# Cross-attention in a two-block network: the queries of heads 2 and 3 as one unit of seven block products, with the sums of token blocks made beside the first four query tiles

## The chip, the cores and the metric

The kernel runs on one core of a Trainium2 chip as one program. The metric is the device time of an execution in microseconds (us); lower is better. The engines that matter are PE (TensorE, the matrix engine), DVE (VectorE), ACT (ScalarE), POOL (GpSimd, used here to issue DMAs that add to what lies in SBUF) and SP (SyncE, which issues the plain loads). Each engine takes its instructions strictly in the order in which the program has them; an instruction that waits for a semaphore holds up all that stand behind it on the same engine.

## The reference, cut to what matters

The network is two blocks in a row on 512 tokens of width 1024. The change touches the cross-attention of the second block, which reads a memory of 256 rows:

```python
def cross_attention(xn, memn, w_q, w_kv, w_o):
    q = (xn @ w_q).reshape(b, s, XATTN_HEADS, XATTN_HEAD_DIM)      # 512 tokens, 4 heads of 256
    k, v = jnp.split(memn @ w_kv, 2, axis=-1)
    ...
    scores = jnp.einsum('bqhd,bkhd->bhqk', q, k).astype(jnp.float32) * (XATTN_HEAD_DIM ** -0.5)
    p = jax.nn.softmax(scores, axis=-1).astype(v.dtype)
    o = jnp.einsum('bhqk,bkhd->bqhd', p, v).reshape(b, s, D_MODEL)
    return o @ w_o
```

The order of the whole is: feed-forward 1, mixer 1, feed-forward 2, mixer 2, cross-attention, squared-ReLU MLP, last norm.

## The kernel before

Activations lie with their features on the 128 partitions and the 512 tokens in the free direction, so the residual is eight tiles `x[0]` to `x[7]` of 128x512, and a linear layer gives its output in tiles of 128 features. Every operand of a matmul is split into a high part and a low part: ACT casts (`L322` for activations, `L269` or `L162` for a weight tile of 128x1024) and DVE subtracts (`L323`, `L270`, `L163`). A product of two split operands takes three matmuls, high by high, high by low and low by high (`mm3`, L278).

A query tile is `q_lin(i)`: `linear` loads one weight tile (SP, 512 KB), splits it, runs 24 matmuls with 512 columns (8 blocks of the depth by 3), and `split_x` splits the result. Tiles 0 and 1 (head 0) have their matmuls in two halves of 256 columns. Two tiles make a head of width 256.

`head(hd)` is a generator. Its first two steps each put the scores of two token blocks into a PSUM tile (`x`, 12 matmuls of 256 columns), take the maximum on DVE (L1377, L1378), the exponential on ACT (L1381), and the reciprocal and the scaling on DVE (L1384, L1387). The third step transposes the probabilities on PE (L1395), splits them, and, for head 0, splits four tiles of V (`L322` and `L323` with 128x512 `a<-a`). The last step multiplies by V (12 matmuls of 512 columns) and splits the two output tiles. `weave` runs one step of the head, then its share of a list of other work, and so on: before, head 0 was woven with tiles 2, 3 and 4, head 1 with tiles 5, 6 and 7, and heads 2 and 3 with the first half of the output projection `w_xo_2`.

The feed-forwards and the MLP use another form of a linear layer, `unit`: a product of 256x256-blocks of the weight with halves of the tokens in seven block products in place of eight (a Strassen form). `twist` makes the sums of token blocks, one `step(k)` for each of four pairs of depth blocks (k, k+4): the two tiles in full (`full`), four adds or subtracts of 128x256 on DVE (L188 to L191), and their splits (`part`, L177 on ACT and L178 on DVE). `end()` splits the last of them into the second half of the tiles `h`. `unit` loads three weight quarters of 512 KB and makes the sums of weight quarters by four DMAs that add in place, issued by POOL (`add_q`, L157). One buffer, `x`, goes through four contents:

```python
        w22 = self.split_q(x)
        self.add_q(x, name, 0, c2)
        ...
        self.product(E, w22, t4, True)
        w = self.split_q(x)
        self.add_q(x, name, 0, c1)
        self.product(C, w, t1, True)
        ...
        w = self.split_q(x)
        self.add_q(x, name, 512, c1)
        self.product(A, w, n2)
```

`split_q` is the cast L162 and the subtract L163; a sum can't be split before the DMA has landed, and the DMA can't start before the split ahead of it has read the buffer. `product` is 24 matmuls of 256 columns (L209). Weight tiles as loaded have 5 buffers (`raw`), split ones 6 (`whl`).

The order of the instructions on each engine is made when the program is built: a scheduler takes them by the order of the code and its own estimates. It is fixed from then on.

Of the kernel before, what the change touches and what calls it, by code (L numbers as in the profile page):

```python
# [14 lines left out]
AF = mybir.ActivationFunctionType  # L15
ALU = mybir.AluOpType
# [64 lines left out]
class Body:  # L81
# [1262 lines left out]
    def xattn(self, h, after):  # L1344
        nc = self.nc
        rs16 = self.const.tile([128, 4], F32, name="rs16")
        nc.vector.tensor_scalar(rs16, self.rs, 1.0 / 16, None, ALU.mult)
        kt, vt = [], []
        for i in range(4):
            t = self.T()  # L1350
            self.load_after(t, self.kv_d[i], self.kv_mark)
            t3 = t.rearrange("p (a c) -> p a c", a=2)
            nc.vector.tensor_tensor(t3, t3, self.rmem.unsqueeze(1).to_broadcast([128, 2, 256]), ALU.mult)
            t = self.split_x(t)
            kt += [self.cut([t], 0, 256), self.cut([t], 256, 512)]
        vr = []
        for i in range(4):
            t = self.T()
            self.load_after(t, self.kv_d[4 + i], self.kv_mark)
            vr.append(t)  # L1360
        om = []
        Q = {}

        def q_lin(i):
            Q[i] = self.split_x(self.linear("w_xq_2", i * 128, h))

        def head(hd):
            q = [Q.pop(2 * hd), Q.pop(2 * hd + 1)]
            es = []
            for bp in range(0, NB, 2):  # L1370
                sp = self.psx()
                for i in range(2):
                    b = bp + i
                    self.mm3(sp[:, i * 256:i * 256 + 256], self.cut(q, b * 128, b * 128 + 128),
                             kt[2 * hd] + kt[2 * hd + 1])
                mx = self.small(8)
                nc.vector.reduce_max(mx[:, 0:2], sp.rearrange("p (b c) -> p b c", b=2), AX.X)  # L1377
                nc.vector.scalar_tensor_tensor(mx[:, 2:4], mx[:, 0:2], -1.0, rs16[:, bp:bp + 2], ALU.mult, ALU.mult)  # L1378
                e = self.T()
                for i in range(2):  # L1380
                    nc.scalar.activation(e[:, i * 256:i * 256 + 256], sp[:, i * 256:i * 256 + 256], AF.Exp,  # L1381
                                         bias=mx[:, 2 + i:3 + i], scale=rs16[:, bp + i:bp + i + 1],
                                         accum_out=mx[:, 4 + i:5 + i])
                nc.vector.reciprocal(mx[:, 6:8], mx[:, 4:6])  # L1384
                for i in range(2):
                    v = e[:, i * 256:i * 256 + 256]
                    nc.vector.tensor_scalar(v, v, mx[:, 6 + i:7 + i], None, ALU.mult)  # L1387
                es.append(e)
                yield
            ptt = []  # L1390
            for kk in range(2):
                pt = self.psx()
                for b in range(NB):
                    o = (b % 2) * 256 + kk * 128
                    nc.tensor.transpose(pt[:, b * 128:b * 128 + 128], es[b // 2][:, o:o + 128], self.ident)  # L1395
                ptt.append(self.split_x(pt))
            while vr:
                vt.append(self.split_x(vr.pop(0)))
            yield
            for dd in range(2):  # L1400
                po = self.psx()
                c = hd * 256 + dd * 128
                self.mm3(po, self.cut([vt[kk * 2 + c // 512] for kk in range(2)], c % 512, c % 512 + 128), ptt)
                om.append(self.split_x(po))

        def qf(*ii):
            return [lambda i=i: q_lin(i) for i in ii]
        for f in qf(0, 1):
            f()
        self.weave([head(0)], qf(2, 3, 4), 4)  # L1410
        self.weave([head(1)], qf(5, 6, 7), 4)
        self.weave([head(2), head(3)],
                   [lambda c0=c0: self.res_full("w_xo_2", 0, om[0:4], None, c0) for c0 in range(0, D, 256)], 4)
        self.res_halves("w_xo_2", 512, om[4:8], None, after)
# [263 lines left out]
```

## Time and profile before

| what | value |
|---|---|
| median of 3 runs | 2084.45 us (2083.64 to 2084.78) |
| profiled execution, its own time | 2080.9 us |
| its span in the profile | 2079.1 us |
| PE busy | 2045.5 us, 98% of the span |
| DVE, ACT, POOL busy | 1473.1 us, 939.6 us, 79.9 us |
| granted TensorE clock, mean | 0.997 |

The profile is of one execution. Times in it count from the start of the span; the 1.8 us between the span and the execution's own time lie around it. Cross-attention's own part (queries, heads, output projection) lies between about 1610 and 1725 us. Instructions of one engine overlap a little in the records, so that the step from one start to the next, not the duration, is what one costs in a row of its kind.

### The profile page before, as it was taken

How to read it: one execution, taken by the hardware profiler on the slowest of the kernel's cores; microseconds unless marked ns; L12 is line 12 of the kernel's file. 1: busy time of each engine (PE TensorE's matmuls, PEld its weight loads, DVE VectorE, ACT ScalarE, POOL GpSimd, SP SyncE). 2: the span in 40 equal slices, each digit the busy share in tenths (PEclk: the TensorE clock that was granted, in tenths of full speed). 3: DMA queues.
4: the chain of work that ended last, by engine and by line, in shares of the span. 5: the costliest groups of instructions: out<-in, count | busy, mean ns of one | idle time of the engine just before them, and what ended most of it. 6: DMA issues, size and time to landing. Idle time of an engine off the chain costs nothing.

```text
span 2079.1 us, 31877 instructions
## 1 busy us (share of the span) xinstructions
PE 2045.5 (98%) x12382; PEld 1796.2 (86%) x12382; DVE 1473.1 (71%) x2993; ACT 939.6 (45%) x1634; POOL 79.9 (4%) x102
## 2 busy tenths in 40 slices
PE   6999999999999999999999999999999999999997
PEld 5888999997777788898999999788889889889987
DVE  6986566788777543487666679889798668566656
ACT  5522444466544322254444446446554446344442
POOL 0000001000000000000101100000000000000000
PEclk9999999999999999999999999999999999999998
DMA  9865466553333343325666643231222314555541
GB/s 327 313 253 162 112 169 149 149 169 117 116 108 118 120 152 122 132 79 139 151 140 171 150 126 125 72 112 42 71 92 71 132 52 121 133 132 142 142 122 41
DMA packets 87784, 277.87 MB, mean 134 GB/s; under 512 B 9937, under 2 KB 15697, under 8 KB 87633
## 3 DMA queue, kind: packets, MB, share of 16 engines
q1 hardware_dynamic: 70352, 223.40, 31.0%
q0 software_dynamic: 12672, 46.14, 13.2%
q10 hardware_dynamic: 4608, 6.29, 0.8%
q8 instruction: 97, 1.59, 0.3%
q14 instruction: 55, 0.44, 0.1%
HBM read 267.41 MB, written 8.39 MB: 133 GB/s over the span
## 4 chain that ended last, share of the span: by engine, by line
PE 93%; DVE 4%; ACT 2%; DMA 1%; issue 1%; SPq 0%; ACTq 0%; DVEq 0%
PE p L278 62%; PE p L209 21%; PE x L1145 1%; PE x L278 1%; PE x L1101 1%; PE x L911 1%; DVE whl L270 1%; PE x L1203 1%; PE x L1086 1%; PE x L900 1%; PE p L727 1%; ACT a L813 1%; PE p L734 1%; DVE a L1272 0%; PE x L869 0%
## 5 line engine op out<-in xcount | busy, mean ns | idle before, releaser
L278 PE MATMUL p<-a,whl 128*128 128x512 f32 (+1 forms) x6624 | 1369.6, 362 | 4.5 <-ACT a L689 1.7
L278 PEld LDWEIGHTS p<-a,whl 128*128 128x128 f32 x6624 | 1096.7, 188 | 200.3 <-issue 10.1
L209 PEld LDWEIGHTS p<-a,whl 128*128 128x128 f32 x3696 | 449.9, 188 | 8.2
L209 PE MATMUL p<-a,whl 128*128 128x256 f32 x3696 | 452.3, 281 | 0.0
L269 ACT CAST whl<-raw 128x1024 fp32r<-128x1024 f32 (+1 forms) x252 | 261.9, 1042 | 264.0 <-PE p L278 174.0
L270 DVE TENSOR_TENSOR whl<-raw,whl 128x1024 fp32r<-128x1024 f32 (+1 forms) x252 | 305.6, 1214 | 86.9 <-ACT whl L269 86.5
L163 DVE TENSOR_TENSOR whl<-raw,whl 128x1024 fp32r<-128x1024 f32 x154 | 187.5, 1223 | 157.2 <-ACT whl L162 156.7
L162 ACT CAST whl<-raw 128x1024 fp32r<-128x1024 f32 x154 | 160.6, 1050 | 226.4 <-PE p L278 99.0
L330 DVE TENSOR_TENSOR a<-a,p 128x512 f32<-128x512 f32 (+1 forms) x120 | 68.7, 579 | 48.7 <-PE p L278 48.3
L331 DVE SCALAR_TENSOR_TENSOR a<-p,mods,a 128x512 f32<-128x512 f32 (+1 forms) x136 | 87.7, 653 | 19.9 <-PE p L278 19.4
L157 POOL DMA_DIRECT2D raw<-in_w_gu x60 | 52.1, 868 | 1142.4 <-DVE whl L163 1126.9
L278 PE MATMUL p<-whl,a 128*128 128x256 f32 (+1 forms) x576 | 77.1, 287 | 0.0
L278 PEld LDWEIGHTS p<-whl,a 128*128 128x128 f32 x576 | 72.0, 188 | 3.0 <-issue 2.2
L418 ACT ACTIVATE q<-a 128x256 f32<-128x256 f32 x120 | 48.5, 413 | 53.1 <-DVE a L330 28.4
L634 DVE CUSTOM_DVE_ANT_0 raw<-raw,a,ct 128x512 f32<-128x512 f32 x56 | 41.5, 749 | 37.3 <-DMA raw<-in_w_ada 37.2
L805 DVE TENSOR_TENSOR a<-a 128x256 fp32r<-128x256 f32 x116 | 45.9, 421 | 11.9 <-ACT a L804 11.8
L157 POOL DMA_DIRECT2D raw<-in_w_up x28 | 24.3, 874 | 749.5 <-DVE s L387 495.0
L420 DVE TENSOR_TENSOR q<-q 128x256 f32<-128x256 f32 x105 | 44.3, 421 | 7.9 <-ACT q L418 7.1
L322 ACT CAST a<-a 128x512 fp32r<-128x512 f32 x51 | 31.3, 620 | 40.1 <-DVE a L756 19.2
L250 DVE TENSOR_TENSOR a<-a,p 128x512 f32<-128x512 f32 x22 | 15.1, 688 | 47.8 <-ACT a L249 47.8
L804 ACT CAST a<-a 128x256 fp32r<-128x256 f32 x116 | 40.7, 404 | 13.0 <-DVE a L773 12.6
L249 ACT COPY a<-p 128x512 f32<-128x512 f32 x22 | 12.9, 587 | 73.8 <-PE p L209 73.8
(262 smaller groups left out, 1751.9 us busy)
## 6 DMA issues: line engine op xcount, KB each, us to landing
raw<-in_w_in SPq DMA_DIRECT2D x86, 512.0 KB, 3.4
raw<-in_w_down SPq DMA_DIRECT2D x76, 512.0 KB, 3.8
raw<-in_w_gu SPq DMA_DIRECT2D x73, 512.0 KB, 4.3
raw<-in_w_gu POOLq DMA_DIRECT2D x60, 512.0 KB, 5.4
raw<-in_w_ada SPq DMA_DIRECT2D x56, 512.0 KB, 3.4
raw<-in_w_up POOLq DMA_DIRECT2D x28, 512.0 KB, 5.3
raw<-in_w_up SPq DMA_DIRECT2D x25, 512.0 KB, 4.1
a<-in_w_ada SPq DMA_DIRECT2D x32, 256.0 KB, 5.2
```

Source lines behind the costliest of these rows:

```text
L157: self.nc.gpsimd.dma_start(t, self.quarter(*q), accum_op=ALU.add)
L162: self.nc.scalar.copy(hi, src)
L163: self.nc.vector.tensor_sub(lo, src, hi.bitcast(F32))
L209: self.nc.tensor.matmul(bank[:, i * 256:i * 256 + 256], w[k][a][:, i * 128:i * 128 + 128], x[k][b], start=first and i == 0 and k == 0 and ...
L269: self.nc.scalar.copy(hi[:, ks, :], src)
L270: self.nc.vector.tensor_sub(lo[:, ks, :], src, hi[:, ks, :].bitcast(F32))
L278: self.nc.tensor.matmul(out, lw[k][a], rx[k][b], start=k == 0 and i == 0, stop=k == n - 1 and i == 2)
L330: return self.nc.vector.tensor_add(x, x, p)
L331: return self.nc.vector.scalar_tensor_tensor(x, p, gt(j), x, ALU.mult, ALU.add)
L418: nc.scalar.activation(q, x[k], AF.Square, scale=s)
L420: nc.vector.tensor_add(q, accs[i], q)
L805: self.nc.vector.tensor_sub(lo, src, hi.bitcast(F32))
```

## The change

The queries of heads 2 and 3 (tiles 4 to 7) are no longer four calls of `q_lin` but one `unit` over the 512 columns. Its result comes back in two pairs of tiles through `evac`, which turns the sign of the second pair (L1417) and splits them. The four steps of `twist` go beside the tiles: steps 0 and 1 follow `q_lin(0)` and `q_lin(1)`, steps 2 and 3 stand at the end of the list that is woven with head 0. The whole unit is the one item woven with head 1. `full` scales a tile of the residual by the norm's gain on ACT (L1411).

```diff
-        for f in qf(0, 1):
-            f()
-        self.weave([head(0)], qf(2, 3, 4), 4)
-        self.weave([head(1)], qf(5, 6, 7), 4)
+
+        def full(k):
+            t = self.T()
+            nc.scalar.activation(t, self.x[k], AF.Identity, scale=self.col("norm_xattn_2", k))
+            return t
+
+        def q_pairs():
+            def evac(blk, hf, t):
+                if blk:
+                    nc.vector.tensor_scalar(t, t, -1.0, None, ALU.mult)
+                self.split_pair(Q, 4 + 2 * blk, hf, t)
+            self.unit("w_xq_2", 512, 768, end(), evac, [])
+        step, end = self.twist(h, full)
+        for i in range(2):
+            q_lin(i)
+            step(i)
+        self.weave([head(0)], qf(2, 3) + [lambda: (step(2), step(3))], 4)
+        self.weave([head(1)], [q_pairs], 4)
```

What stands on the engines was moved by the scheduler too. First ACT, from the split of query tile 0 (`L322 CAST a<-p`) to the first exponentials of head 0 (L1381). Before:

```order
L269 CAST whl<-raw 128x1024
L322 CAST a<-p 128x512 x2
L269 CAST whl<-raw 128x1024
L1381 ACTIVATE a,s<-x,s,rs_15358 128x256 x2
L322 CAST a<-p 128x512
L1381 ACTIVATE a,s<-x,s,rs_15358 128x256 x2
```

And now:

```order
L162 CAST whl<-raw 128x1024
L322 CAST a<-p 128x512
L1411 ACTIVATE a<-a,ct 128x512 x2
L177 CAST a<-a 128x512
L322 CAST a<-p 128x512
L162 CAST whl<-raw 128x1024
L1411 ACTIVATE a<-a,ct 128x512 x2
L177 CAST a<-a 128x256
L177 CAST a<-a 128x512
L177 CAST a<-a 128x256
L177 CAST a<-a 128x512
L1381 ACTIVATE a,s<-x,s,rs_15358 128x256 x2
```

The two casts L162 here are those of the second and the third content of the buffer `x`, each of which waits for a DMA of POOL that adds; they and the work of steps 0 and 1 now stand ahead of head 0's exponentials.

On PE, at the end of query tile 3 (24 matmuls of 512 columns, `p<-a,whl`), head 0's transposes L1395 follow, as before; behind them stood the next query tile:

```order
L278 MATMUL p<-a,whl 128x512 x24
L1395 MATMUL x<-ident,a 128x128 x8
L278 MATMUL p<-a,whl 128x512 x24
L278 MATMUL x<-a 128x512 x12
```

Now the products A and B of the unit (L209) stand behind the first transpose, then head 0's product with V (`x<-a 128x512`), then products E and C:

```order
L278 MATMUL p<-a,whl 128x512 x21
L1395 MATMUL x<-ident,a 128x128
L209 MATMUL p<-a,whl 128x256
L1395 MATMUL x<-ident,a 128x128
L209 MATMUL p<-a,whl 128x256 x8
L1395 MATMUL x<-ident,a 128x128 x2
L209 MATMUL p<-a,whl 128x256 x2
L1395 MATMUL x<-ident,a 128x128 x4
L209 MATMUL p<-a,whl 128x256 x30
L278 MATMUL x<-a 128x512 x4
L209 MATMUL p<-a,whl 128x256 x4
L278 MATMUL x<-a 128x512 x2
```

The first transpose still follows the same matmuls, with nothing of the unit moved ahead of it.

On DVE, behind the splits of head 0's probabilities (`L323 a<-x,a`), the four splits of V were followed by those of a query tile and of the next weight tile. Now steps 2 and 3 of `twist` follow them:

```order
L323 TENSOR_TENSOR a<-a 128x512 x4
L188 TENSOR_TENSOR a<-a 128x256
L189 SCALAR_TENSOR_TENSOR a<-a 128x256
L190 TENSOR_TENSOR a<-a 128x256
L191 SCALAR_TENSOR_TENSOR a<-a 128x256
L178 TENSOR_TENSOR a<-a 128x256
L270 TENSOR_TENSOR whl<-raw,whl 128x1024
L178 TENSOR_TENSOR a<-a 128x512
```

Here L270 is the split of the first weight tile of `w_xo_2`; the second run of L188 to L191 (step 3) and the last three L178 come right behind these rows. The products C and E need the L178 of all four steps.

## Rows read from the trace of the kernel before

**Rows 1.** The page: the whole span; busy us, share, instructions of an engine.

```profile
span 2079.1 us, 31877 instructions
PE 2045.5 (98%) x12382; PEld 1796.2 (86%) x12382; DVE 1473.1 (71%) x2993; ACT 939.6 (45%) x1634; POOL 79.9 (4%) x102
```

**Rows 2.** Stretches: length, then busy us of PE, PEld, DVE, ACT, POOL, PE clock, DMA.

```profile
1600.00:1622.30 22.30, 22.30 (x173) 21.48 (x172) 20.74 (x51) 12.27 (x23) 0.00 (x0) 1.00 0.50 170
1622.30:1700.00 77.70, 77.70 (x401) 65.12 (x401) 44.22 (x83) 32.44 (x68) 0.00 (x0) 1.00 0.21 71
```

**Rows 3.** Timeline of PE in cross-attention: start, us, engine, line, form, count.

```profile
1626.32 5.72 PE L278 MATMUL p<-a,whl 128*128 128x512 f32 x24
1631.88 1.03 PE L1395 MATMUL x<-ident,a 128*128 128x128 f32 x8
1632.68 5.83 PE L278 MATMUL p<-a,whl 128*128 128x512 f32 x24
```

**Rows 4.** Timeline of PE in the MLP: a unit's product among other tiles.

```profile
1769.83 2.98 PE L209 MATMUL p<-a,whl 128*128 128x256 f32 x24
1772.65 5.70 PE L278 MATMUL p<-a,whl 128*128 128x512 f32 x24
```

**Rows 5.** Timelines of ACT and DVE before the first scores of head 0.

```profile
1611.77 1.22 DVE L270 TENSOR_TENSOR whl<-raw,whl 128x1024 fp32r<-128x1024 f32 x1
...
1618.12 1.05 ACT L269 CAST whl<-raw 128x1024 fp32r<-128x1024 f32 x1 [0.71 <-PE p L278]
1619.08 1.07 ACT L322 CAST a<-p 128x512 fp32r<-128x512 f32 x2
```

**Rows 6.** Timelines of ACT, DVE and POOL around one adding DMA of feed-forward 1.

```profile
213.65 1.05 ACT L162 CAST whl<-raw 128x1024 fp32r<-128x1024 f32 x1 [2.41 <-PE p L278]
214.74 1.23 DVE L163 TENSOR_TENSOR whl<-raw,whl 128x1024 fp32r<-128x1024 f32 x1 [0.44 <-ACT whl L162]
216.26 0.86 POOL L157 DMA_DIRECT2D raw<-in_w_gu  x1 [15.81 <-DVE whl L163]
221.67 1.05 ACT L162 CAST whl<-raw 128x1024 fp32r<-128x1024 f32 x1 [6.45 <-DMA raw<-in_w_gu]
```

**Rows 7.** Line L157 over the span; then the DMA issues of 936.5 to 940 us.

```profile
DMA to landing us min/median/max: 5.2/5.4/9.0
...
raw<-in_w_gu POOLq DMA_DIRECT2D x2, 512.0 KB, 5.9
```

**Rows 8.** Timelines of DVE and ACT at head 0's second pair of token blocks.

```profile
1629.16 0.15 DVE L1378 SCALAR_TENSOR_TENSOR s<-s,rs 128x2 f32<-128x2 f32 x1
1629.41 0.56 ACT L1381 ACTIVATE a<-x,s,rs 128x256 f32<-128x256 f32 x1 [1.63 <-DVE s L1378]
1630.64 0.17 DVE L1384 RECIPROCAL s<-s 128x2 f32<-128x2 f32 x1 [1.33 <-ACT a L1381]
1630.84 0.61 DVE L1387 TENSOR_SCALAR a<-a,s 128x256 f32<-128x256 f32 x2
```

**Rows 9.** Timelines of DVE and ACT: four splits of V, then sums and splits in the MLP.

```profile
1634.47 2.21 ACT L322 CAST a<-a 128x512 fp32r<-128x512 f32 x4
1635.99 2.49 DVE L323 TENSOR_TENSOR a<-a 128x512 fp32r<-128x512 f32 x4
...
1746.16 0.42 DVE L190 TENSOR_TENSOR a<-a 128x256 f32<-128x256 f32 x1
1746.49 0.42 DVE L191 SCALAR_TENSOR_TENSOR a<-a 128x256 f32<-128x256 f32 x1
...
1754.24 1.22 DVE L270 TENSOR_TENSOR whl<-raw,whl 128x1024 fp32r<-128x1024 f32 x1
1755.37 0.68 DVE L178 TENSOR_TENSOR a<-a 128x512 fp32r<-128x512 f32 x1
```

**Rows 10.** Line L1439 (the MLP's `full`), its forms; duration min/median/max in ns.

```profile
L1439 ACT ACTIVATE a<-a,ct x8: 707/711/723, 1723.6 to 1750.4; 128x512 f32<-128x512 f32 x8
```

**Rows 11.** Timeline of PE at idle stretches; then stretches: PE busy, clock, DMA.

```profile
52.26 0.70 PE L447 MATMUL x<-t,ones 128*128 128x256 f32 x2 [2.40 <-DVE t L441]
2059.21 0.70 PE L447 MATMUL x<-t,ones 128*128 128x256 f32 x2
2067.66 0.58 PE L427 MATMUL x<-ones,q 128*128 128x1 f32 x4 [1.54 <-DVE q L420]
2071.12 1.22 PE L447 MATMUL x<-t,ones 128*128 128x256 f32 x2 [2.88 <-DVE t L441]
...
52.00:56.00 4.00, 3.74 (x17) 1.00 1.00 361
2069.00:2071.00 2.00, 0.00 (x0) 0.50 0.00 0
```

## The prediction

> **What bounds the kernel now.** I read the page first: PE is busy for 2045.5 of 2079.1 us [rows 1], so a matmul saved is time saved, and a wait of PE is time lost, wherever they lie. Then the stretch that the change touches. From 1622.3 to 1700 us PE is busy for all of 77.70 us; DVE is busy for 44.22 and ACT for 32.44 [rows 2]. There is thus nothing to win from a wait here, only from fewer columns, and DVE has 33 us of air, ACT 45. Just ahead of it, from 1600 to 1622.3, DVE is busy for 20.74 of 22.30 us: what is put there is not free. Last the order of the changed kernel, because each engine goes through its list in order and a single late cast holds up all behind it.
>
> **What goes and what comes on PE.** Four query tiles of 24 matmuls with 512 columns go: 24 of them take 1631.88 - 1626.32 = 5.56 us [rows 3], 231.7 ns each, so 96 take 22.24 us. Seven products of 24 matmuls with 256 columns come: 24 take 1772.65 - 1769.83 = 2.82 us [rows 4], 117.5 ns each, so 168 take 19.74 us. PE saves 2.50 us. This is the whole gain, 0.12% of the time. Nothing else on PE changes in number.
>
> **What DVE and ACT get.** Step by step from the rows of their kind: 16 sums of 128x256 at 0.33 us from start to start [rows 9], 5.3 us; splits of sums, six of 128x512 at 0.6 and four of 256 columns at 0.33, 4.9 us; three more weight splits at 1.13, 3.4 us; four additions of bank contents and two turns of sign, some 3.6 us; the splits of the queries themselves 0.3 us more. That is some 17 us on DVE. ACT gets eight `full` of 0.71 us [rows 10], three more casts of 1.05, splits and copies: some 16 us. Both would fit into the air of the whole stretch. They cost nothing where PE has other matmuls in front of it, and their full length where PE needs them next; so the question is where they stand. I went through the lists of the four engines with the durations above and found two places where PE has to wait.
>
> **First place: head 0's first transpose.** Before, PE arrives at L1395 at 1631.88 [rows 3], and the last scaling of the probabilities had started at 1630.84 and taken 0.61 [rows 8]: ready with 0.4 us to spare. Now two casts of the buffer `x` stand ahead of the exponentials on ACT, each behind a DMA that adds.
> - The first content of `x` is split by DVE where a query tile's weight was, at 1611.77 [rows 5], since DVE's list is the same up to there. POOL issues 216.26 - 214.74 = 1.52 us after such a subtract starts [rows 6], at 1613.3. To landing it is 5.4 us in the median, 5.2 at best, 9.0 at worst, and 5.9 where two adds and plain loads run together [rows 7]. The second add (into `y`) follows 1.9 us later here, beside loads of K, V and `w_xo_2`, so I take 5.7: the second content can be cast at 1619.0. Before, the cast at that place of ACT's list began at 1618.12 [rows 5].
> - From that cast to the cast of the third content is a round of cast, subtract, issue and landing: 221.67 - 213.65 = 8.02 us [rows 6]. So ACT reaches it at 1627.0, having had some 3 us of other work, and stands idle for the rest. Queued behind it are step 1, the last splits of step 0 and head 0's exponentials; PE waits for those.
> - Behind it: DVE's subtract starts 1.1 later and takes 1.13 (1629.2); L188, L190, L189 (1630.2); the maximum, 0.6, and L191, 0.33 (1631.2); an L178, 0.6 (1631.8), then L1378 and 0.25 us later the exponential [rows 8], at 1632.05. The reciprocal can come 1.23 later, but DVE has another maximum, an L178 of 512 columns and two of 256 ahead of it (1633.95); 0.2 for the reciprocal and 0.3 for the first scaling make 1634.5.
>
> PE arrives at 1631.9 as before, for up to there it has the same matmuls. It waits **2.6 us**. With the bounds of the landing it is 2.1 (5.2 us) to 5.9 (9.0 us).
>
> **Second place: product C, its last depth block.** From 1634.5 PE has eight transposes, A and B, head 0's product with V, and the first blocks of E and C: 0.8 + 5.64 + 2.8 + 0.7 + 1.1 = 11.0 us, so it is at C's block 3 at 1645.6. On DVE the second pair of probabilities is scaled by 1636.2. Then come the split of tile 3 (0.6), of the fourth sum of weights (1.13), of two probability tiles (1.2): 1639.1. The split of `x`'s fourth content takes a buffer that A frees at 1638.2; cast and subtract end at 1640.65. Four splits of V at 0.6 [rows 9]: 1643.05. Step 2, four times 0.33 and an L178 of 256 columns: 1644.75. The split of the first tile of `w_xo_2` takes the buffer that B frees at 1643.9, so its cast ends at 1645.1 and its subtract at 1646.3. An L178 (0.6) and step 3 (1.33 and an L178 of 0.42): 1648.65. C needs this one; E's last L178 ends at 1650.0, just as PE gets there. PE waits **3.0 us**, in two pieces with one matmul between. If no cast waited for a buffer DVE would be 0.8 earlier (2.2); a late landing moves both engines alike and changes little here.
>
> **Later places.** The query halves come out of the unit at some 1656 (first pair) to 1673; heads 2 and 3 begin at 1676 behind products of `w_xo_2`, so they are covered. Head 1's transposes meet their probabilities within 0.3 us. I put 0.4 us for all short waits together. SP's list has the same places as before for the three loads of the unit, and the loads of `w_xo_2` and `w_up_2` come up to 10 us later but are needed only from 1700 us on; POOL had nothing else to do here. Behind the stretch PE is busy without a wait again, so nothing is given back.
>
> **The sum.** -2.50 + 2.6 + 3.0 + 0.4 = +3.5 us: the profiled 2080.9 would become 2084.4, the median 2084.45 becomes **2088.0 us**. The profiled execution is 3.6 us below the median of the runs; the difference is carried over. About 0.2%, 4.2 us, is what a measurement here can tell from no change, so this is a small loss that the bound just hides.
>
> **The clock.** In this trace PE stood idle for 2.40 us until 52.26 and the granted clock stayed 1.00, the level of 2.4 GHz; at the end of the program, after 1.54 us without work, 0.58 us of work and more idle time, it is 0.50, the level of 1.2 GHz, and a pair of matmuls takes 1.22 in place of 0.70 us [rows 11]. The forecast waits of 2.6 and 3.0 us are longer than the one that did nothing. The Trainium skill (TensorE: Matmul & The Clock Gate, section "Part 1: The HAM clock gate") says that the throttled level is the default and only recent activity releases it, which speaks against this change; by it a wait of such a length may or may not be answered, and the two rows bear out that both happen.
>
> **Rivals.**
> - *No wait* (not slower): the adds land early and the lists of ACT and DVE run ahead of PE. Then only the 2.50 us count: 2081.95. For it speaks the 33 us of air; against it that the first transpose had 0.4 us to spare and two rounds of an add now stand ahead of it. Even the fastest landing leaves 2.1 + 3.0. Chance 0.10.
> - *The clock falls in one of the waits* (slower): the place is the first transpose, or block 3 of C. At the low level work takes 1.22/0.70 = 1.74 times as long [rows 11], and A alone would be 2.1 us longer, A and B 4.2. I take 2.1, as A's 24 matmuls are dense: +5.6, 2090.0. It decides as soon as a wait is answered at all; 2.40 us was not. Chance 0.20.
> - *The first add lands late* (slower): its 512 KB run beside the K, V and `w_xo_2` loads. At 9.0 us the first wait is 5.9: +6.8, 2091.2. From 6.4 us on the loss is over 0.2%. Chance 0.15.
> - *The forecast*, 0.55, itself between +2.2 and +4.9 (2086.6 to 2089.3).
>
> **How the numbers follow.** Slower by over 0.2% (above 2088.6) are the clock, the late add and the upper part of the forecast, which I put at 0.12: 0.47. Faster by over 0.2% (below 2080.3) would need 1.7 us more than PE saves; 0.02 out of the first rival. The rest, 0.51, is within 0.2%. The range of 8 in 10 runs from 2084.0, which leaves out most of the first rival, to 2091.5, which takes in the clock and most of the late add.
>
> **What would show it.** Right: 168 matmuls L209 from some 1633 to 1668 us; an idle stretch of PE of 2 to 3 us before the first L1395, released by DVE L1387, and one of about 3 us in all before an L209, released by ACT L177 and DVE L178; ACT idle before the second L162 of that part, released by the DMA of `w_xq`; an end of cross-attention 3 to 4 us later. Wrong: PE busy throughout, then the first rival; a granted clock under 1.00 behind one of the waits, then the second; a wait of 5 us and more before L1395, then the third. The step that I trust least is the landing of the first add.

## The result, and the profile after

The changed kernel takes 2095.23 us in the median (2093.16 to 2098.88, 4 runs), the kernel before 2084.32 us beside it (4 runs). The ratio is 1.0058, with a 95% interval of 1.0046 to 1.0069: slower by 0.6%; the medians are 10.9 us apart. The forecast was 2088.0 us, with a range of 2084.0 to 2091.5. The direction of the sum was right and its size was not: the time lies above the range.

The page of the changed kernel, its span and the busy time of each engine, answers to [rows 1]:

```profile
span 2091.4 us, 32108 instructions
PE 2048.9 (98%) x12454; PEld 1802.0 (86%) x12454; DVE 1490.1 (71%) x3032; ACT 954.4 (46%) x1662; POOL 83.3 (4%) x106
```

72 matmuls more, as 168 for 96 make; 17 us more on DVE and 15 on ACT, where some 17 and 16 were forecast. PE's busy time hides the loss: it rose by 3.4 us although the new matmuls are cheaper.

To find the place, take the first small matmul L427 of cross-attention and the first one of the MLP. Before, they start at 1596.37 and 1713.62 us, 117.25 apart; now at 1597.03 and 1725.30, **128.27** apart:

```profile
1596.37 0.28 PE L427 MATMUL x<-ones,q 128*128 128x1 f32 x2
1713.62 0.28 PE L427 MATMUL x<-ones,q 128*128 128x1 f32 x2
...
1597.03 0.28 PE L427 MATMUL x<-ones,q 128*128 128x1 f32 x2
1725.30 0.28 PE L427 MATMUL x<-ones,q 128*128 128x1 f32 x2
```

These 11.02 us are nearly all of the 12.3 us between the two spans; the rest, 0.7 us ahead of the stretch and 0.6 behind it, is of the size by which executions of one kernel differ. PE has four waits in this stretch where it had none. The timeline of PE (start, us, engine, line, form, count, and in brackets the idle time before and what ended it) shows both places that were forecast:

```profile
1623.31 0.39 PE L278 MATMUL x<-a 128*128 128x256 f32 x1 [0.42 <-DVE a L323]
...
1628.57 5.04 PE L278 MATMUL p<-a,whl 128*128 128x512 f32 x21
1638.82 0.45 PE L1395 MATMUL x<-ident,a 128*128 128x128 f32 x1 [5.21 <-DVE a L1387]
...
1649.72 2.18 PE L209 MATMUL p<-a,whl 128*128 128x256 f32 x17
1653.90 0.38 PE L209 MATMUL p<-a,whl 128*128 128x256 f32 x1 [2.00 <-ACT a L177]
1655.00 3.01 PE L209 MATMUL p<-a,whl 128*128 128x256 f32 x17 [0.72 <-DVE a L178]
1657.81 2.44 PE L278 MATMUL x<-a 128*128 128x256 f32 x12
1660.09 1.93 PE L209 MATMUL p<-a,whl 128*128 128x256 f32 x15
```

The wait ahead of head 0's first transpose is 5.2 us where 2.6 were forecast; the one in product C is 2.0 and 0.7 us in two pieces with one matmul between, where 3.0 were. Why the first is so long stands in the timelines of POOL and ACT:

```profile
1614.86 0.88 POOL L157 DMA_DIRECT2D raw<-in_w_xq  x1 [378.76 <-DVE s L384]
...
1620.35 1.05 ACT L162 CAST whl<-raw 128x1024 fp32r<-128x1024 f32 x1 [2.00 <-DMA raw<-in_w_xq]
...
1622.95 0.86 POOL L157 DMA_DIRECT2D raw<-in_w_xq  x1 [6.01 <-DVE whl L163]
...
1631.34 1.05 ACT L162 CAST whl<-raw 128x1024 fp32r<-128x1024 f32 x1 [5.75 <-DMA raw<-in_w_xq]
...
1636.30 0.56 ACT L1381 ACTIVATE a<-x,s,rs 128x256 f32<-128x256 f32 x1
```

These are the two adds into `x` that come first; they are called the first and the second add from here on. (A third one, into `y`, which the prediction counts as the second, is issued between them.) The first add is issued at 1614.86 and its sum is cast at 1620.35: 5.49 us. The second is issued at 1622.95, and ACT stands idle until its sum can be cast at 1631.34: 8.39 us. Head 0's exponentials are in ACT's list behind that cast, and start at 1636.30.

The windows (length, busy us of PE, granted clock, DMA share, GB/s) show what came on top:

```profile
1630.00:1634.00 4.00, 3.61 (x16) 1.00 0.00 0
1634.00:1638.00 4.00, 0.00 (x0) 0.73 0.63 97
1638.00:1642.00 4.00, 3.18 (x15) 0.50 0.18 34
1642.00:1646.00 4.00, 4.00 (x34) 0.92 0.41 131
...
1654.00:1658.00 4.00, 3.28 (x19) 0.79 0.27 108
1658.00:1662.00 4.00, 4.00 (x30) 0.78 0.00 0
```

During the first wait and behind the second the granted clock falls from 1.00, the level of 2.4 GHz, towards 0.50, the level of 1.2 GHz: it is 0.50 from 1638 to 1642, and 0.79 and 0.78 in the two windows from 1654 on. PE works through these us at the low level before the clock is back: work is slow just when it is late.

### The profile page after: what moved, and what is told of

It is laid out like the page before. It is cut to its first block, busy times and chain, and to the rows that moved or that the text cites. A ratio compares the mean times of both kernels' runs of the same rounds, so it can differ in the third digit from the quotient of the medians.

```text
span 2091.4 us, 32108 instructions
## 1 busy us (share of the span) xinstructions
PE 2048.9 (98%) x12454; PEld 1802.0 (86%) x12454; DVE 1490.1 (71%) x3032; ACT 954.4 (46%) x1662; POOL 83.3 (4%) x106
## 3 DMA queue, kind: packets, MB, share of 16 engines
HBM read 268.98 MB, written 8.39 MB: 133 GB/s over the span
## 5 line engine op out<-in xcount | busy, mean ns | idle before, releaser
L278 PE MATMUL p<-a,whl 128*128 128x512 f32 (+1 forms) x6528 | 1348.3, 362 | 4.3 <-ACT a L689 1.7
L209 PEld LDWEIGHTS p<-a,whl 128*128 128x128 f32 x3864 | 473.0, 189 | 12.1 <-ACT a L177 2.2
L209 PE MATMUL p<-a,whl 128*128 128x256 f32 x3864 | 477.2, 282 | 2.8 <-ACT a L177 2.0
L269 ACT CAST whl<-raw 128x1024 fp32r<-128x1024 f32 (+1 forms) x248 | 257.6, 1042 | 252.7 <-PE p L278 169.5
L270 DVE TENSOR_TENSOR whl<-raw,whl 128x1024 fp32r<-128x1024 f32 (+1 forms) x248 | 300.6, 1214 | 84.4 <-ACT whl L269 83.9
L163 DVE TENSOR_TENSOR whl<-raw,whl 128x1024 fp32r<-128x1024 f32 x161 | 196.0, 1223 | 164.9 <-ACT whl L162 164.5
L162 ACT CAST whl<-raw 128x1024 fp32r<-128x1024 f32 x161 | 167.8, 1050 | 234.3 <-PE p L278 100.5
L157 POOL DMA_DIRECT2D raw<-in_w_gu x60 | 52.0, 867 | 1142.9 <-DVE whl L163 1127.4
L322 ACT CAST a<-a 128x512 fp32r<-128x512 f32 x51 | 31.2, 618 | 41.8 <-DVE a L756 19.9
L888 ACT ACTIVATE a<-a,s 128x256 f32<-128x256 f32 (+1 forms) x64 | 30.1, 471 | 28.2 <-DVE s L883 16.5
```

Source lines behind the costliest of these rows:

```text
L157: self.nc.gpsimd.dma_start(t, self.quarter(*q), accum_op=ALU.add)
L162: self.nc.scalar.copy(hi, src)
L163: self.nc.vector.tensor_sub(lo, src, hi.bitcast(F32))
L209: self.nc.tensor.matmul(bank[:, i * 256:i * 256 + 256], w[k][a][:, i * 128:i * 128 + 128], x[k][b], start=first and i == 0 and k == 0 and ...
L269: self.nc.scalar.copy(hi[:, ks, :], src)
L270: self.nc.vector.tensor_sub(lo[:, ks, :], src, hi[:, ks, :].bitcast(F32))
```

## The experiments

Three theories stood against each other. **Queue**: the adds' landings hold up ACT's list, and with it the exponentials and PE. **Work**: DVE and ACT simply have too much to do ahead of PE. **Clock**: a part of the loss is work at the low level behind a wait. Each run was timed beside the kernel before on the same chip. Not all were on one chip, so the ratios compare better than the medians; each is known to a little over 0.1%, some 2.5 us. Line numbers move by some lines where an edit adds lines. "Stretch" is from cross-attention's first small matmul to the MLP's, as above, in the profiled execution; "waits" is the sum of PE's in it.

| run | median us | ratio to before, 95% | stretch us | waits us |
|---|---|---|---|---|
| before | 2082.85 to 2084.32 | | 117.25 | 0 |
| changed | 2095.23 | 1.0058 (1.0046 to 1.0069) | 128.27 | 8.3 |
| sums alone | 2083.81 | 1.0000 (0.9991 to 1.0008) | 117.65 | 0 |
| no adds | 2087.78 | 1.0022 (1.0013 to 1.0032) | 121.43 | 2.7 |
| one V tile | 2090.16 | 1.0036 (1.0023 to 1.0049) | 120.98 | 4.1 |
| tile 3 twice | 2092.65 | 1.0047 (1.0032 to 1.0062) | 125.71 | 2.2 |
| exponentials first | 2090.14 | 1.0032 (1.0019 to 1.0044) | 124.82 | 4.9 |
| sums earlier | 2093.44 | 1.0042 (1.0029 to 1.0055) | 125.67 | 6.1 |
| both: exponentials first, sums earlier | 2089.03 | 1.0030 (1.0019 to 1.0040) | 121.37 | 3.8 |
| both, and V's loads late | 2090.74 | 1.0032 (1.0021 to 1.0044) | 123.41 | 5.0 |
| both, and V's splits first | 2083.33 | 1.0003 (0.9995 to 1.0012) | 116.83 | 0.7 |
| all lists ordered | 2083.87 | 1.0007 (0.9998 to 1.0016) | 117.58 | 2.0 |

**The sums alone.** The kernel before, with the sums made and split, read by nobody:

```diff
+        step, end = self.twist(h, full)
+        for i in range(2):
+            q_lin(i)
+            step(i)
-        self.weave([head(0)], qf(2, 3, 4), 4)
+        self.weave([head(0)], qf(2, 3) + [lambda: (step(2), step(3))] + qf(4), 4)
```

> The kernel before, with the four steps of twist put where the change has them (steps 0 and 1 behind tiles 0 and 1, steps 2 and 3 in head 0's list); the sums are made and split but nothing reads them, and tiles 4 to 7 are computed as before. So DVE and ACT get the sums (some 9 and 9 us), but no add and no product of the unit. If what stops PE is ACT's list standing behind the adds' landings, no wait of more than 0.5 us appears ahead of head 0's first transpose and the time is that of before plus at most 2: 2083 to 2086. If the sums' own work is what delays the exponentials and the splits, the first transpose waits 2 us or more, and the time is 2087 or more.

Measured: 2083.81 us, ratio 1.0000, and not one wait of PE in the stretch. The sums of all four steps fit beside the tiles as long as no DMA stands in the same list and nothing needs them soon.

**The unit without its adds.** The four adding DMAs are left out, so the products use plain weight quarters:

```diff
     def add_q(self, t, *q):
+        if self.phase == "xat":
+            return
```

> The changed kernel without the four adding DMAs (the sums of weights are left out, so that the queries of heads 2 and 3 are not the reference's); casts, subtracts, sums of token blocks and matmuls stay, in the same order. The queue theory expects ACT not to wait at the third content, the exponentials of head 0 some 5.5 us earlier, no wait of PE before the first transpose and the clock at 1.00 there: 5.4 and 1.9 us less, 2088. The work theory (the 17 us that DVE gets for sums and splits, which stand ahead of the exponentials, hold them back) expects the wait to stay near 5 us: 2095. The wait in product C stays in both, with the clock's fall behind it.

Measured: 2087.78 us, as the queue theory had it. PE's timeline of this run:

```profile
1634.94 0.27 PE L1397 MATMUL x<-ident,a 128*128 128x128 f32 x1
...
1644.07 2.18 PE L211 MATMUL p<-a,whl 128*128 128x256 f32 x17
1648.24 0.38 PE L211 MATMUL p<-a,whl 128*128 128x256 f32 x1 [2.00 <-ACT a L179]
1649.34 4.00 PE L211 MATMUL p<-a,whl 128*128 128x256 f32 x17 [0.72 <-DVE a L180]
1653.14 2.58 PE L280 MATMUL x<-a 128*128 128x256 f32 x12
```

The first wait is gone, the second is there to the hundredth: it has nothing to do with the adds. And the work between the first transpose and the 17 matmuls of C, the same in both kernels, takes 1644.07 - 1634.94 = 9.13 us at clock 1.00 here, and 1649.72 - 1638.82 = 10.90 us in the changed kernel: the fall of the clock costs 1.77 us at the first place.

**Tile 3 twice.** More work for PE ahead of the first transpose; tile 3 is computed twice into the same bank:

```diff
             self.mm3(p[:, 0:n], wt, h)
+            if (name, c0) == ("w_xq_2", 384):
+                self.mm3(p[:, 0:n], wt, h)
```

> The changed kernel with the 24 matmuls of query tile 3 done twice: 5.56 us of work for PE exactly where it waits 5.4 us before head 0's first transpose. The queue theory (that wait is ended by ACT, which stands behind the cast of the third content of x until the second add has landed) expects no wait there over 0.3 us, a granted clock of 1.00 from there to product C, and, as the added work only fills the wait, a gain of what the low clock costs at the first place, about 1.9 us: 2093.3. If the clock costs nothing: 2095.2. If PE itself sets the end there and the wait is paid back later: 5.6 more, 2100.8. The wait of about 3 us in product C stays in all of them.

Measured: 2092.65 us, that is 5.56 us of work more than the changed kernel and, in the profiled executions, a stretch 2.56 us *shorter* (the intervals of the two ratios overlap; the third expectation, 2100.8, is far outside). PE has no wait ahead of the first transpose, and in the trace the clock stays 1.00 there. The 1.77 us that the clock cost at this place are most of the 2.56; the rest is the wait in C, 0.9 us shorter here. Useless work in place of the wait cost less than the wait and the slow work behind it.

**One V tile.** V's first tile is loaded and used in place of all four, so three loads of 256 KB go:

```diff
-        for i in range(4):
-            t = self.T()
-            self.load_after(t, self.kv_d[4 + i], self.kv_mark)
-            vr.append(t)
+        t = self.T()
+        self.load_after(t, self.kv_d[4], self.kv_mark)
+        vr += [t] * 4
```

> The changed kernel with one tile of V loaded and used for all four (the output is not the reference's): 768 KB less in flight when the second add is issued. If the loads of V slow that add, it lands in 5.4 to 6 us in place of 8.4, the wait before the first transpose falls from 5.4 to about 2.5, and the time by 3 us, or by 5 if the clock then holds: 2090 to 2092.5. If the adds slow each other, or plain loads don't matter, the landing stays over 8 us and the time at 2095.

Measured: 2090.16 us, inside what contention with the loads was to give. Timelines of POOL, ACT and PE:

```profile
1625.91 0.86 POOL L157 DMA_DIRECT2D raw<-in_w_xq  x1 [6.01 <-DVE whl L163]
...
1631.38 1.05 ACT L162 CAST whl<-raw 128x1024 fp32r<-128x1024 f32 x1 [1.59 <-DMA raw<-in_w_xq]
...
1638.53 0.70 PE L1394 MATMUL x<-ident,a 128*128 128x128 f32 x4 [0.53 <-DVE a L1386]
...
1651.62 0.38 PE L209 MATMUL p<-a,whl 128*128 128x256 f32 x1 [1.58 <-ACT a L177]
1652.19 2.69 PE L209 MATMUL p<-a,whl 128*128 128x256 f32 x20 [0.19 <-DVE a L178]
1654.72 1.58 PE L278 MATMUL x<-a 128*128 128x256 f32 x12
1656.13 1.60 PE L209 MATMUL p<-a,whl 128*128 128x256 f32 x12
```

From the second add's issue to the cast of its sum it is now 5.47 us, not 8.39, and the wait of 5.2 us is 0.5. In the changed kernel V's four loads, issued from 1617.15 us on and 8.5 us in flight in the median, run beside this add; the busy share of the 16 DMA engines from 1623 to 1629 is 1.05. The Trainium skill (DMA: Bandwidth & Descriptors, "Issuing engines are not separate DMA queues") says that DMAs issued by different engines end up on the same 16 DMA engines and interleave there. The trace agrees: 8.39 against 5.47 us.

How late the add lands is not fixed, though. With all of V's loads issued ahead of it, it landed after 6.4 to 8.4 us in the profiles of six runs here (8.3 in the changed kernel, 6.9 with tile 3 twice, 7.2 with the sums earlier); with one V tile after 5.4, and also after 5.3 where it was issued 2.3 us later in the stretch, when V's loads were nearly done (the run with all lists ordered). Nor are V's loads all of it: the add into `y`, issued 1.2 us behind the first one, landed after 8.3 to 9.1 us in every run with adds, with one V tile too, and with V's loads issued only 7 us behind it (the run with V's loads late). Whether the first add or the other loads slow that one is not shown.

**Exponentials first.** ACT casts the third content of `x` only behind head 0's last exponential; an order on one engine, no new wait:

```diff
         w = self.split_q(x)
+        if self.phase == "xat":
+            self.tc.add_manual_dep(self.cast.ins, self.exps[3].ins.name, ...)
         self.add_q(x, name, 512, c1)
```

> The changed kernel with one ordering more and nothing else: ACT casts the third content of x behind the last exponential of head 0. The queue theory expects the wait before the first transpose to be gone or under 0.5 us, with the clock at 1.00: up to 7.3 us less. Later contents of x come later, and the cast of the fourth may now hold the splits of V on ACT, 2 to 3 us: 2088 to 2090.5. The work theory expects a wait of 3 us or more before the transpose, since both steps of sums still stand ahead of the exponentials: 2093 or above.

Measured: 2090.14 us, 5.1 less than the changed kernel by the medians and 3.45 less by the stretch, with all its work, loads and adds. The wait before the first transpose is gone: the queue theory holds for the first place. Its waits of PE (us in total, times, longest) show where the rest stands:

```profile
PE p L209 <- ACT a L177: 2.0, 1, 2.0
PE x L283 <- ACT a L327: 1.8, 2, 1.3
PE p L209 <- DVE a L178: 0.7, 1, 0.7
PE x L283 <- DVE a L328: 0.4, 1, 0.4
```

The wait in C is unmoved, and one for V's splits (L327) has come up behind the first.

**Sums earlier.** Step 2 behind tile 2 and step 3 behind tile 3:

```diff
-        self.weave([head(0)], qf(2, 3) + [lambda: (step(2), step(3))], 4)
+        self.weave([head(0)], [lambda: (q_lin(2), step(2)),
+                               lambda: (q_lin(3), step(3)), lambda: None], 4)
```

> The changed kernel with step 2 of twist behind tile 2 and step 3 behind tile 3, in place of both behind tile 3 and head 0's third step; on DVE they now stand ahead of the four splits of V. If the second loss is the place of the sums behind V's splits in DVE's list, the wait ahead of product C (2.0 and 0.7 us, released by ACT L177 and DVE L178) goes, and with it the fall of the clock behind it (some 1.5): 4.2 less than the changed kernel, 2091; the wait of 5 us ahead of the first transpose stays. If DVE and ACT simply have too much to do ahead of C, whatever the order, the same 2 to 3 us come back as a wait for V's splits or for the second pair of probabilities, and the time stays at 2094 to 2096.

Measured: 2093.44 us, between the two expectations. The trace tells more than the time:

```profile
PE x L1395 <- DVE a L1387: 4.1, 1, 4.1
PE x L278 <- DVE a L323: 0.7, 2, 0.4
PE x L278 <- ACT a L322: 0.6, 1, 0.6
PE p L278 <- ACT a L322: 0.4, 1, 0.4
PE p L209 <- DVE a L178: 0.3, 1, 0.3
```

The wait ahead of the first transpose stays, as expected; it is 4.1 and not 5.2 us since the second add landed after 7.2 us in this profile. The wait in C went from 2.7 to 0.3, so its cause was the place of the sums; but some 1.3 us came back as waits for V's splits and what hangs on them (L322, L323), which now stand behind the sums.

**Both together**, exponentials first and sums earlier:

> As the run before, and ACT casts the third content of the buffer x only behind head 0's last exponential. If the two waits are two separate faults of order, both go: the changed kernel less 5.1 (by the run with exponentials first) and less 4.2, 2086, within 0.2% of before. If there is too much work, the waits move to the fourth content of x and V's splits, and the time is that of the run with exponentials first or more: 2090 to 2092.

Measured: 2089.03 us, nearer to the second expectation. Neither of the old waits is left; five waits of 3.4 us in all stand in head 0's product with V and right behind it (the 3.9 of a later expectation counts the 0.4 ahead of the scores too). ACT's and PE's timelines:

```profile
1646.09 1.05 ACT L162 CAST whl<-raw 128x1024 fp32r<-128x1024 f32 x1 [1.68 <-DMA raw<-in_w_xq]
...
1647.52 1.05 ACT L274 CAST whl<-raw 128x1024 fp32r<-128x1024 f32 x1
1648.47 0.62 ACT L327 CAST a<-a 128x512 fp32r<-128x512 f32 x1
1648.99 1.05 ACT L274 CAST whl<-raw 128x1024 fp32r<-128x1024 f32 x1
...
1649.14 1.20 PE L283 MATMUL x<-a 128*128 128x512 f32 x4 [1.22 <-ACT a L327]
```

V's splits (L327 `a<-a`) stand behind the fourth content of `x`, for whose DMA ACT waits 1.68 us, and between casts of `w_xo_2` (L274), which PE needs only behind that product.

**V's loads late.** As the last, with V's loads issued behind the second piece of head 0's queries:

```diff
+        def load_v():
+            for i in range(4):
...
-        ... lambda: (q_lin(3), step(3)), lambda: None], 4)
+        ... lambda: (load_v(), q_lin(3), step(3)), lambda: None], 4)
```

> As the run before, and V's four loads are issued behind the second piece of head 0's queries instead of with K's, so that the second adding DMA runs with fewer loads beside it. If loads beside an adding DMA make it land late, the landing of the second add falls from 8.4 to 5.5 to 6.5 us, the fourth content's cast waits less, and the time is 2082 to 2085, at or below before. If the landing does not depend on them, the time is that of the run before within 1 us, or above it where V itself now comes late.

Measured: 2090.74 us, no gain, so the expectation failed. The trace says that the run did not do what it was for: SP issued the four loads from 1627.75 us on, and the second add went out at 1627.30, so the two ran side by side as before, and that add landed after 8.2 us. What this run tells is only that V and the sums came later: PE waited 2.0 us in the products and 1.7 for a split of V. It tells nothing on V's loads beside the second add.

**V's splits first.** As both together, and ACT casts the fourth content of `x` and the weights of `w_xo_2` behind V's last split:

```diff
+                if name == "w_xo_2":
+                    self.behind(cast, self.v_cast, "V first")
...
-        self.product(C, self.split_q(x), b22)
+        w = self.split_q(x)
+        if self.phase == "xat":
+            self.behind(self.cast, self.v_cast, "V first")
+        self.product(C, w, b22)
```

> As the run with exponentials first and the sums earlier, and ACT casts the fourth content of x and the weights of w_xo_2 only behind the four splits of V. That run's trace has its waits (3.9 us) ahead of head 0's product with V, whose splits stand behind the fourth content (which waits for its DMA) and three splits of w_xo_2. If their place in the lists is the cause, the waits go from 3.9 to at most 1 us and the time falls by some 3 to 2086. If DVE simply has more between 1640 and 1650 than fits ahead of PE, a wait of 2 us or more stays, ahead of E, C or the product with V, and the time falls by at most 1.5: 2087.5 to 2089.

Measured: 2083.33 us, ratio 1.0003 (0.9995 to 1.0012): all of the loss is gone, more than either expectation gave. The arithmetic, the four adds and the loads are the same; only the order of the instructions differs from the changed kernel, on PE too, whose list the scheduler moved along with those of ACT and DVE. The second add still landed after 6.8 us, but nothing that PE needs soon stood behind it. Two waits of PE are left, 0.42 and 0.33 us, and its unit shows what the products cost:

```profile
1637.47 6.92 PE L214 MATMUL p<-a,whl 128*128 128x256 f32 x56
1644.22 2.94 PE L293 MATMUL x<-a 128*128 128x512 f32 x12
...
1654.51 3.09 PE L214 MATMUL p<-a,whl 128*128 128x256 f32 x24
1657.43 0.38 PE L1412 MATMUL x<-ident,a 128*128 128x128 f32 x2
```

From start to start, 56 take 6.75 us and 24 take 2.92. The seven runs of L214 together take 20.40 us for 168, 121.4 ns each, not the 117.5 of [rows 4].

**All lists ordered.** Further in the same direction: the second content behind head 0's query splits, the third behind the last sums, V's splits and head 0's product with V behind product C:

```diff
+            self.behind(self.cast, self.q_cast, "queries first")
...
+            self.behind(self.cast, self.sum_cast, "sums first")
...
-            self.unit("w_xq_2", 512, 768, end(), evac, [])
+            self.unit("w_xq_2", 512, 768, tw, evac, [no, lambda: next(g0, None), no, no])
```

Here `g0` is head 0, whose last step (V's splits and the product with V) is called inside the unit.

> The changed kernel with the lists put in the order in which PE needs the results: query splits of head 0 ahead of the second content of x, exponentials ahead of the third, the sums of step 2 and 3 behind tiles 2 and 3 and ahead of the third content, head 0's product with V and V's splits behind product C, the fourth content and w_xo_2 behind V's splits. The arithmetic and the four adds are the same. If every loss was one of order, PE has no wait of over 0.5 us, the clock stays at 1.00, and what is left is the saving of 2.5: 2081 to 2083, at or a little below before. If the unit's work or its adds cost in themselves, 3 us and more stay: 2086 or more.

Measured: 2083.87 us, ratio 1.0007 (0.9998 to 1.0016): no better, and above the 2081 to 2083 that went with no wait of over 0.5 us. The 0.4 us ahead of the scores went, but waits of 1.2 us (product A for the copy of its bank, L236) and 0.8 us (a weight of `w_xo_2`) came. Of the two versions that lose nothing, neither is shown to be faster than before.

## Why the prediction was wrong

By its own terms, in us; measured waits are from start to start, which is some 0.2 to 0.4 more than the idle time that the rows give.

| term | forecast | measured |
|---|---|---|
| 168 matmuls for 96 | -2.50 | -1.84 |
| wait ahead of the first transpose | +2.6 | +5.4 |
| wait in product C | +3.0 | +3.2 |
| short waits | +0.4 | +0.6 |
| clock | none (a rival, 2.1 once) | +1.8 and +1.5 |
| sum | +3.5 | +10.7, of 11.0 |

The second value for the clock: 17 matmuls of C and 12 of scores take 1660.09 - 1655.00 = 5.09 us in the changed kernel; at clock 1.00, by 1654.72 - 1652.19 = 2.53 us for 20 in the run with one V tile and 1.41 for 12 scores, they take 3.56, so the low clock costs 1.53. The saving is measured in the run with V's splits first, from 22.24 to 20.40 us.

**The step that failed** is "from that cast to the cast of the third content is a round of cast, subtract, issue and landing: 8.02 us". It was 10.99 us (1620.35 to 1631.34), because the second add landed after 8.39 us and not after the 5.4 that [rows 6] has in it. These 2.97 us make up the 2.8 by which the first wait came out too long. The text gave bounds of 5.2 and 9.0 to the landing of the *first* add, which it trusted least, and put the second at the median without a bound, although V's loads lie beside it; the one V tile and the six landings of 6.4 to 8.4 us show that the median did not hold there, and that 8.39 is near the upper end of what such a landing takes. The first add landed after 5.49 us, within 0.2 of what was taken; only its issue was late, 2.42 us behind the start of its subtract (1612.44 in DVE's timeline) and not 1.52; why it was late is open (the row names a later DVE instruction, L384, the rows of other runs a DMA). This adds little to the wait, as PE itself came to the transpose some 0.9 us later in the stretch. The third rival (first wait 5.9, 2091.2) named the right size, place and sign, but the wrong add.

**The second failure** is the clock. It stood as a rival of its own with a chance of 0.20, as if it could come only in place of a long wait and only once. In the trace a late add and a fall of the clock came together, and at both places. 2.40 us without a fall [rows 11] said little on a wait of 5.2. The Trainium skill (TensorE: Matmul & The Clock Gate, "Part 1: The HAM clock gate"), weighed in the forecast, holds that only recent activity keeps the throttled level away; at both waits the changed kernel's trace agrees, with 0.50 and 0.78; a run in which the level held is shown in the last section. Had the two terms been added, the sum would have been 6.8 for the late add and 2.1 for each fall, some 11 us.

**A term that was mis-sized**: a product beside the MLP's tiles takes 2.82 us for 24 [rows 4], those in this stretch 2.87 to 2.95 (run with V's splits first). Why is open.

**What was right**: the saving and the waits lie where the text put them, with the releasers that it named; the second wait was within 0.2 us, down to its two pieces; and from the cast of the third content to the first transpose 7.5 us were forecast and 7.48 measured (1631.34 to 1638.82). That DVE and ACT have air enough for the sums is shown by the sums alone. That the order of the lists, not the amount of work, sets the loss is shown by the run with V's splits first. What stays open is why no version gains: it saves 1.84 us on PE and has some 1.1 us of waits from start to start left, and a rest of 0.7 us, 0.03%, is less than a measurement here can tell (in the profiled executions its stretch is 0.42 us shorter than before).

## What to carry to other kernels

An instruction that waits for a DMA is a wall in its engine's list: look up what stands behind it, and put what PE needs next ahead of it. When a forecast has a chain of DMAs, give every landing in it its bounds, by what else is being loaded in the same us, and not only the first one, and add what a wait does to the clock to the wait. When one wait is removed, name the next splits in the list: here the loss moved from the exponentials to the sums and to V's splits, and was gone only when all three stood in the order in which PE asks for them.

## What the hardware showed that was not expected

Like waits were answered differently by the clock. In the run with tile 3 twice, PE waited 1.58 and 0.19 us in product C, and the granted clock of the next us fell:

```profile
1650.00:1654.00 4.00, 2.24 (x18) 1.00 0.10 22
1654.00:1658.00 4.00, 4.00 (x21) 0.58 0.27 110
```

In the run with one V tile it waited 1.58 and 0.19 us at the same matmuls, and the clock stayed:

```profile
1650.00:1654.00 4.00, 2.23 (x17) 1.00 0.37 131
1654.00:1658.00 4.00, 4.00 (x36) 1.00 0.02 4
```

The 20 matmuls behind the waits took 3.99 us in the first (1653.98 to 1657.97) and 2.53 in the second. In the run with both orders five waits of 3.4 us in all, between 1648 and 1655.5, left the clock at 1.00, and in the run without adds 2.0 and 0.7 us took it to 0.50. The price differs too. Behind the same waits of 2.0 and 0.7 us in product C, the 17 matmuls and 12 of scores took 5.09 us in the changed kernel, 6.21 without adds (1649.34 to 1655.55) and 6.28 with exponentials first (1652.04 to 1658.32), against 3.56 at clock 1.00. The length of a wait alone does not tell, and no run here shows what does.

An adding DMA of 512 KB landed after 5.1 to 9.1 us in these runs; what runs beside it is a part of the cause, as the run with one V tile shows. The loads of 256 KB of V and of the last part of K landed after 8.4 us in the median beside the adds, 5.4 before and 4.9 without the adds.
